# Windowed attention on one core: value products of three blocks in one run, a written order for the tensor engine, and the query projection spread over the blocks

## Chip, core and metric

The kernel is one program on one core of a Trainium2 chip. The core has a tensor engine (PE, whose weight loads the profile lists apart as PEld), a vector engine (DVE), a scalar engine (ACT), GpSimd (POOL), and a sync engine (SP) whose queue issues the DMA transfers here. Each engine works through its own instructions in order, and semaphores tie them together. Operands lie in the on-chip memory SBUF; PE writes to PSUM, eight banks of 128 partitions by 512 floats, and DVE and ACT read PSUM back.

The metric is device time of one execution in microseconds, the median of several runs. The profile is of one execution, with the time of every instruction.

## The reference

Two sequences, a prompt of 256 positions and a sample of 512, go through a network of two layers of width 1024. Layer 0 mixes with a chunked mLSTM, layer 1 with windowed attention, and each is followed by a feed-forward part with a short convolution. All is float32. The change lies in the attention of layer 1:

```python
def swa_mixer(h, w_in, sink, rel_bias, w_out):
    proj = h @ w_in
    q, k, v = ...        # 16 query heads, 4 key/value heads, 64 wide
    ...
    def block(i):        # 128 query positions, keys of up to 384 positions around them
        s = jnp.einsum('bqkgd,bckd->bkgqc', qb, kb).astype(jnp.float32) * scale + bias
        s = jnp.where(valid, s, -jnp.inf)
        m = jnp.maximum(jnp.max(s, axis=-1, keepdims=True), sink_l)
        p = jnp.exp(s - m)
        denom = jnp.sum(p, axis=-1, keepdims=True) + jnp.exp(sink_l - m)
        ob = jnp.einsum('bkgqc,bckd->bqkgd', p / denom, vb.astype(jnp.float32))
        return ob.astype(h.dtype)
    ...
    return outs @ w_out
```

## The kernel before

The two sequences stand side by side as 768 columns, the prompt in columns 0 to 255 and the sample in 256 to 767. Float32 matrices that go through PE at full rate are split into a high and a low part in a reduced format, and a product is three matmuls: high by high, high by low, low by high (line 268, `gemmT_steps`). A projection of 128 output rows over one sequence is eight steps of three matmuls, 512 columns wide for the sample and 256 for the prompt, into one PSUM bank.

The attention stage is `swa` (line 814). It projects the keys and the first half of the queries (`window`, line 283), multiplies a one-hot matrix with the table of relative biases (line 862) and sends the result to memory, from where the bias rows `bt` are loaded for each pair of heads (line 913). The values are projected by `gemmN` (line 304) into `vn`. The queries come in eight halves of 128 rows, one for each pair of heads j: weights are loaded in halves of 512 KB (`raw`) and split by ACT (`whi`, line 232) and DVE (`wlo`, line 233). What a projection leaves in PSUM is scaled and split for each of the two heads by ACT (line 852) and DVE (line 853).

The attention itself is a list of 48 blocks: eight pairs of heads, for each the four blocks of the sample and the two of the prompt. A block has 128 query positions and 256 or 384 keys. It goes through three functions:

- `scores` (line 906): four matmuls, two for each head, into two banks; DVE adds the bias and takes the maximum (line 929), ACT takes the exponentials with their sum (line 938), DVE forms the reciprocal of the sum (line 943), POOL scales the probabilities `t` (line 945).
- `flip` (line 947): PE transposes the probabilities by 128 columns at a time (line 953), four or six transposes, and ACT and DVE copy them to `pt` (lines 957 and 955).
- `values` (line 959): products of the transposed probabilities with `vn`. Each head of a pair fills 64 of the 128 rows of the result, so these matmuls use 64 columns of the array, all others 128. A bank `po` collects the blocks of one sequence, and ACT copies it to `att` behind the last of them (line 974).

`pack` (line 885) splits a finished pair of heads for the output projection, ACT the high part and DVE the low one. It writes over `hh` and `hl`, the input that the query projections read.

The loop at line 979 writes, for step x, the scores of block x, three steps of the query projection of a later unit, the flip of block x-3 (`LAG`, line 36) and the values of block x-4. It does not fix the order on the engines. A scheduler does: it takes instructions by their place in the program and by when its own estimate of times has them ready, engine by engine. So the matmuls stand on PE in another order than they are written, and matmuls of the output projection (`out_proj`, line 559), which comes next in the program, stand among the blocks as well.

PSUM is held as two groups of four banks. `ps` (line 207) serves the projections. `pa` (line 213) serves scores, flips, and `po`.

SBUF holds six large tiles (`slab`): keys, query halves, attention outputs, and, toward the end of the stage, the residual input that the output projection adds to, loaded in six transfers of 512 KB.

Of the kernel before, what the change touches and what calls it, by code (L numbers as in the profile page):

```python
# [10 lines left out]
F32 = mybir.dt.float32  # L11
# [4 lines left out]
P = 128  # L16
# [17 lines left out]
NPART = FC // 2  # L34
EPS = 1e-6
LAG = 3

HELD = float("inf")
BIG = 1.0e30
# [24 lines left out]
U_AIN = 20  # L64
# [77 lines left out]
class Net:  # L142
# [671 lines left out]
    def swa(self, pool):  # L814
# [26 lines left out]
        def queries(u, c):  # L841
            if c == 0:
                qts[u] = self.slab([P, 4, T], R)
            qt = qts[u]

            def evac(q, o):
                s0, s1 = SEQS[q]
                for e in range(2):
                    src = o[64 * e : 64 * e + 64]
                    hi = qt[64 * e : 64 * e + 64, 2 * c + e, s0:s1]  # L850
                    lo = qt[64 - 64 * e : 128 - 64 * e, 2 * c + e, s0:s1]
                    nc.scalar.activation(hi, src, AF.Copy, scale=0.125)
                    nc.vector.scalar_tensor_tensor(lo, src, 0.125, hi.bitcast(F32), ALU.mult, ALU.subtract)

            return evac

        items = [(w, keys(c)) for c, w in self.halves(U_AIN)]
        rest = self.halves(U_AIN + 2)
# [9 lines left out]
        v = pool.tile([P, T // P, 256], F32, name="vn")  # L868
        self.gemmN(U_AIN + 1, lambda t, o: nc.scalar.copy(v[:, t], o))

        _, w = next(rest)
        evac = queries(0, 1)
        for q in range(2):
            evac(q, self.gemmT(w, q))
        att = [self.slab([P, 4, T]) for _ in range(2)]

        def project(u):
            for c, w in self.halves(U_AIN + 2 + u):
                evac = queries(u, c)
                for q in range(2):  # L880
                    for o in self.gemmT_steps(w, q):
                        yield
                    evac(q, o)

        def pack(c):
            for s0, s1 in SEQS:
                self.fp_copy_split(self.hh[:, c, s0:s1], self.hl[:, c, s0:s1], att[c // 4][:, c % 4, s0:s1])
# [4 lines left out]
        blocks = []  # L892
        for j in range(8):
            for q, (s0, s1) in enumerate(SEQS):
                n = (s1 - s0) // P
                for i in range(n):
                    b = Block()
# [6 lines left out]
        po = {}  # L904

        def scores(b):
            j, kv = b.j, b.j // 2
            if j not in bias:
                bias[j] = []
                for e in range(2):  # L910
                    bt = pool.tile([P, 384], F32, tag="bt", name=self.nm("bt"), bufs=3)
                    row = bd[2 * j + e : 2 * j + e + 1]
                    nc.sync.dma_start(
                        bt, bass.AP(tensor=row.tensor, offset=row.offset, ap=[[1, P], [1, 384]])
                    )
                    bias[j].append(bt)
            co = (b.lo - b.i + 1) * P
            k0 = b.s0 + b.lo * P
            q0 = b.s0 + b.i * P
            K = b.K  # L920
            b.t = t = pool.tile([P, 2, 384], F32, tag="t", name=self.nm("t"), bufs=4)
            st = pool.tile([P, 8], F32, tag="st", name=self.nm("st"), bufs=6)
            rm, mx, sm, rd = (st[:, 2 * z : 2 * z + 2] for z in range(4))
            for e in range(2):
                S = self.pa()[:, :K]
                qb = qts[j // 2][:, 2 * (j % 2) + e, q0 : q0 + P]
                for z in range(2):
                    self.mm(S, qb, kk[kv // 2][:, kv % 2, z, k0 : k0 + K], z == 0, z == 1)
                nc.vector.tensor_tensor_reduce(
                    out=t[:, e, :K], in0=S, in1=bias[j][e][:, 384 - co - K : 384 - co][:, ::-1], op0=ALU.add, op1=ALU.max,  # L930
                    scale=1.0, scalar=-BIG, accum_out=rm[:, e : e + 1],
                )
            sk = self.cst(SK + 2 * j, 2)
            nc.vector.tensor_tensor(mx, rm, sk, ALU.max)
            nc.vector.tensor_tensor(rd, sk, mx, ALU.subtract)
            nc.vector.tensor_scalar(mx, mx, -1.0, None, ALU.mult)
            for e in range(2):
                nc.scalar.activation(
                    t[:, e, :K], t[:, e, :K], AF.Exp, bias=mx[:, e : e + 1], accum_out=sm[:, e : e + 1]
                )  # L940
            nc.scalar.activation(rd, rd, AF.Exp)
            nc.vector.tensor_tensor(rd, rd, sm, ALU.add)
            nc.vector.reciprocal(rd, rd)
            for e in range(2):
                nc.gpsimd.tensor_scalar(t[:, e, :K], t[:, e, :K], rd[:, e : e + 1], 1.0, ALU.mult, ALU.mult)

        def flip(b):
            b.pt = pool.tile([P, 2, 384], F32, tag="pt", name=self.nm("pt"), bufs=3)
            for e in range(2):
                pp = self.pa()[:, : b.K]  # L950
                for kb in range(b.nk):
                    ks = slice(kb * P, (kb + 1) * P)
                    nc.tensor.transpose(pp[:, ks], b.t[:, e, ks], self.ident)  # L953
                if e:
                    nc.vector.tensor_copy(b.pt[:, e, : b.K], pp)
                else:
                    nc.scalar.copy(b.pt[:, e, : b.K], pp)

        def values(b):
            j, kv = b.j, b.j // 2  # L960
            if b.i == 0:
                po[j, b.q] = self.pa()
            o = po[j, b.q]
            for kb in range(b.nk):
                for e in range(2):
                    self.mm(
                        o[64 * e : 64 * e + 64, b.i * P : (b.i + 1) * P],
                        v[:, b.s0 // P + b.lo + kb, kv * 64 : (kv + 1) * 64],
                        b.pt[:, e, kb * P : (kb + 1) * P],
                        kb == 0,  # L970
                        kb == b.nk - 1,
                    )
            if b.i == b.n - 1:
                nc.scalar.copy(att[j // 4][:, j % 4, b.s0 : b.s1], o[:, : b.s1 - b.s0])

        fill = iter(())
        nb = len(blocks)
        packed = 0
        for x in range(nb + LAG + 1):
            if x < nb:  # L980
                if x % 12 == 0:
                    for _ in fill:
                        pass
                    u = x // 12 + 1
                    fill = project(u) if u < 4 else iter(())
                scores(blocks[x])
            for _ in range(3):
                next(fill, None)
            if LAG <= x < nb + LAG:
                flip(blocks[x - LAG])  # L990
            if x > LAG:
                b = blocks[x - LAG - 1]
                values(b)
                if x >= 36 and b.i == b.n - 1 and b.q == 1:
                    while packed <= b.j:
                        pack(packed)
                        packed += 1
        return None


# [596 lines left out]
```

## Time and profile before

| | us |
|---|---|
| median of 3 runs | 1900.98 |
| lowest and highest of them | 1899.35, 1902.82 |
| the profiled execution | 1904.33 |
| its span, first to last instruction | 1902.5 |

| engine | busy us | share of the span | instructions |
|---|---|---|---|
| PE | 1830.7 | 96% | 11270 |
| PEld | 1667.5 | 88% | 11270 |
| DVE | 1399.1 | 74% | 2296 |
| ACT | 910.3 | 48% | 1832 |
| POOL | 490.3 | 26% | 387 |

The attention stage runs from about 1080 to 1290 us; the output projection and the feed-forward part of layer 1 follow to the end.

How to read the lines: a group is named by source line, engine, operation and out<-in tiles (buffer numbers left out), with partitions by elements; behind the count stand busy time and mean duration, then the idle time of the engine before the group and what ended it. In a timeline the first two columns are start and length. A matmul's length covers its way through the array, and the next one starts before it ends. So PE counts as busy nearly all the time, and its pace is read from one start to the next. A float32 product with both operands unsplit, such as a value product, is recorded as two matmuls.

### The profile page before, as it was taken

Reading aid. Unit: us, or ns where it says so; the run is one execution under the profiler, and the core shown is the slowest. Engines: PE = TensorE matmul, PEld = TensorE weight load, DVE = VectorE, ACT = ScalarE, POOL = GpSimd, SP = SyncE. Lnnn points to the kernel's source line nnn. Section 1 sums busy time; section 2 is a strip of 40 time slices with the busy share of each in tenths; the row PEclk is TensorE's granted clock in tenths of the full one; section 3 lists DMA queues with packets and bytes.
Section 4 is the critical chain, followed back from the end, with each engine's and each line's share of the span. In section 5 each row is a group of like instructions: output and inputs, shape, how many; then the busy total and the mean of one; then the engine's idle time right before and its main releaser. Section 6 shows DMA issues by size and latency. Waiting matters only on the chain. (4 is left out here: it accounts for less than half of the span.)

```text
span 1902.5 us, 29053 instructions
## 1 busy us (share of the span) xinstructions
PE 1830.7 (96%) x11270; PEld 1667.5 (88%) x11270; DVE 1399.1 (74%) x2296; ACT 910.3 (48%) x1832; POOL 490.3 (26%) x387
## 2 busy tenths in 40 slices
PE   7999999999999999999999999999989999999997
PEld 4987887888998999999999998779979999999997
DVE  4665577686689777777777755875997777777776
ACT  3444433444455444444444555774565444444443
POOL 2101001031023333333332211340133333333322
PEclk9999999999999999999999999999999999999998
DMA  8343556556312222222223221122222222222211
GB/s 330 109 134 121 167 181 195 168 164 208 99 53 69 68 67 67 67 67 67 67 67 100 90 89 43 44 85 89 78 78 78 67 67 67 67 67 67 67 34 67
DMA packets 64245, 184.48 MB, mean 97 GB/s; under 512 B 6167, under 2 KB 23831, under 8 KB 64108
## 3 DMA queue, kind: packets, MB, share of 16 engines
q1 hardware_dynamic: 64108, 182.63, 29.6%
q8 instruction: 88, 1.44, 0.3%
q14 instruction: 49, 0.40, 0.1%
HBM read 176.17 MB, written 6.43 MB: 96 GB/s over the span
## 5 line engine op out<-in xcount | busy, mean ns | idle before, releaser
L232 ACT CAST whi<-raw 128x1024 fp32r<-128x1024 f32 x237 | 248.5, 1049 | 412.2 <-PE pa L226 197.9
L233 DVE TENSOR_TENSOR wlo<-raw,whi 128x1024 fp32r<-128x1024 f32 x237 | 325.2, 1373 | 123.9 <-ACT whi L232 122.8
L226 PE MATMUL pa<-slab,whi 128*128 128x256 f32 (+1 forms) x1472 | 348.8, 334 | 4.7 <-DVE slab L557 4.5
L226 PEld LDWEIGHTS pa<-slab,whi 128*128 128x128 f32 x1472 | 254.0, 191 | 31.6 <-DVE slab L557 6.4
L557 DVE SCALAR_TENSOR_TENSOR slab<-pa,mod,slab 128x256 f32<-128x256 f32 (+1 forms) x368 | 207.6, 591 | 72.7 <-PE pa L226 72.3
L226 PE MATMUL pa<-slab,wlo 128*128 128x256 f32 (+1 forms) x736 | 235.4, 332 | 0.0
L226 PE MATMUL ps<-zh,whi 128*128 128x256 f32 (+2 forms) x688 | 228.8, 336 | 4.6 <-ACT whi L232 3.5
L226 PE MATMUL ps<-zh,wlo 128*128 128x256 f32 (+2 forms) x688 | 229.1, 336 | 4.0 <-DVE wlo L233 4.0
L226 PE MATMUL ps<-zl,whi 128*128 128x256 f32 (+2 forms) x688 | 229.4, 335 | 0.4 <-DVE zl L520 0.4
L1114 PE MATMUL ps<-zh,whi 128*128 128x384 f32 x504 | 171.1, 339 | 15.8 <-ACT ps L1169 14.5
L1115 PE MATMUL ps<-zl,whi 128*128 128x384 f32 x504 | 169.7, 337 | 0.8 <-DVE zl L1072 0.8
L1116 PE MATMUL ps<-zh,wlo 128*128 128x384 f32 x504 | 168.9, 335 | 0.0
L226 PEld LDWEIGHTS pa<-slab,wlo 128*128 128x128 f32 x736 | 140.2, 191 | 13.4 <-DVE wlo L233 0.9
L226 PEld LDWEIGHTS ps<-zh,whi 128*128 128x128 f32 x688 | 132.0, 193 | 17.5 <-ACT whi L232 5.1
L226 PEld LDWEIGHTS ps<-zh,wlo 128*128 128x128 f32 x688 | 132.2, 192 | 15.1 <-DVE wlo L233 4.8
L226 PEld LDWEIGHTS ps<-zl,whi 128*128 128x128 f32 x688 | 132.2, 193 | 11.5 <-issue 1.7
L1367 POOL TENSOR_TENSOR slab<-slab 128x772 f32<-128x772 f32 x44 | 83.7, 1903 | 205.0 <-DVE slab L1341 193.5
L1145 POOL TENSOR_TENSOR raw<-raw,raw 128x512 f32<-128x512 f32 x40 | 52.3, 1308 | 293.9 <-DVE wlo L233 244.3
L1340 DVE SCALAR_TENSOR_TENSOR slab<-slab,cstt,slab 128x771 f32<-128x771 f32 x88 | 104.8, 1193 | 26.9 <-ACT slab L1338 26.9
L1341 DVE SCALAR_TENSOR_TENSOR slab<-slab,cstt,slab 128x771 f32<-128x771 f32 x88 | 120.2, 1365 | 0.8
L476 DVE SCALAR_TENSOR_TENSOR ada<-raw,silc,ada 128x1024 f32<-128x1024 f32 x84 | 112.4, 1369 | 7.7 <-DMA raw<-in_adaln_w_dram 7.5
L1114 PEld LDWEIGHTS ps<-zh,whi 128*128 128x128 f32 x504 | 94.6, 188 | 23.9 <-ACT ps L1169 19.7
(291 smaller groups left out, 4155.0 us busy)
## 6 DMA issues: line engine op xcount, KB each, us to landing
raw<-in_w_dram SPq DMA_DIRECT2D x208, 512.0 KB, 3.7
raw<-in_adaln_w_dram SPq DMA_DIRECT2D x84, 512.0 KB, 4.3
slab<-in_x_dram SPq DMA_DIRECT2D x12, 512.0 KB, 7.6
slab<-in_adaln_w_dram SPq DMA_DIRECT2D x12, 512.0 KB, 10.3
slab<-mrows SPq DMA_DIRECT2D x8, 384.0 KB, 5.7
xs<-slab SPq DMA_DIRECT2D x6, 512.0 KB, 3.7
bt<-brow SPq DMA_DIRECT2D x16, 192.0 KB, 3.1
slab<-xs SPq DMA_DIRECT2D x6, 512.0 KB, 9.0
```

The source lines that it names most:

```text
L226: self.nc.tensor.matmul(out, lhsT, rhs, start=start, stop=stop)
L232: nc.scalar.copy(hi, src)
L233: return nc.vector.tensor_tensor(lo, src, hi.bitcast(F32), ALU.subtract)
L476: stt(acc[:, s], row, w, acc[:, s], ALU.mult, ALU.add)
L557: self.nc.vector.scalar_tensor_tensor(x, o, self.mod[l][:, gc + c, q : q + 1], x, ALU.mult, ALU.add)
L1114: mm(o, wh[:, k], hi[k], start=start and k == 0, stop=False, skip_group_check=True)
L1115: mm(o, wh[:, k], lo[k], start=False, stop=False, skip_group_check=True)
L1116: mm(o, wl[:, k], hi[k], start=False, stop=k == 3, skip_group_check=True)
L1145: tt(q[0], q[2], q[0], ALU.subtract)
L1340: stt(y[:, 1:], u[:, :-1], w(0), y[:, 1:], ALU.mult, ALU.add)
L1341: stt(y[:, :-1], u[:, 1:], w(2), y[:, :-1], ALU.mult, ALU.add)
L1367: nc.gpsimd.tensor_tensor(y, y, yrow[:, j], ALU.mult)
```

## The change

- The loop's PE instructions stand in a block with a written order: PE takes them as the program lists them, and no other PE work comes between. The other engines are still ordered by the scheduler.
- The values of three blocks are written together, in every third step, right behind that step's flip.
- The bank `po` comes from `ps`, the projections' group, in place of `pa`.
- `pt` has five buffers in place of three.
- The seven halves of the queries behind the first are one generator of 113 steps with the weights fetched and split one half ahead. The second half, which was projected ahead of the loop, is part of it. Step x of the loop runs it on until 6 + (x+1)*107/40 steps (rounded down, at most 113) are done, so it ends at x = 39.
- The call of `gemmT` for the second half goes, and with it its `tick`, which hands time to pending normalizations; at that point there is none.

In the written order of the changed kernel a step is: the projection's matmuls, the scores of block x, the flip of block x-3, and every third step the values of blocks x-6 to x-4. Value products form 16 runs on PE where they form 74 before. Before, 63 matmuls of the output projection stand ahead of the last value product; after the change none does. POOL has the same instructions in the same order. On SP the same 386 transfers are issued, eleven weight loads, bias rows and residual loads among them in another order.

```diff
-        _, w = next(rest)
-        evac = queries(0, 1)
-        for q in range(2):
-            evac(q, self.gemmT(w, q))
         att = [self.slab([P, 4, T]) for _ in range(2)]
 
-        def project(u):
-            for c, w in self.halves(U_AIN + 2 + u):
-                evac = queries(u, c)
+        def weights():
+            yield next(rest)[1]
+            for u in range(1, 4):
+                for _, w in self.halves(U_AIN + 2 + u):
+                    yield w
+
+        def project():
+
+            ws = weights()
+            nxt = next(ws)
+            for j in range(1, 8):
+                w, nxt = nxt, next(ws, None)
+                evac = queries(j // 2, j % 2)
                 for q in range(2):
                     for o in self.gemmT_steps(w, q):
                         yield
...
-            b.pt = pool.tile([P, 2, 384], F32, tag="pt", name=self.nm("pt"), bufs=3)
+            b.pt = pool.tile([P, 2, 384], F32, tag="pt", name=self.nm("pt"), bufs=5)
...
-                po[j, b.q] = self.pa()
+                po[j, b.q] = self.ps()
...
-        fill = iter(())
+        fill = project()
         nb = len(blocks)
-        packed = 0
-        for x in range(nb + LAG + 1):
-            if x < nb:
-                if x % 12 == 0:
-                    for _ in fill:
-                        pass
-                    u = x // 12 + 1
-                    fill = project(u) if u < 4 else iter(())
-                scores(blocks[x])
-            for _ in range(3):
-                next(fill, None)
-            if LAG <= x < nb + LAG:
-                flip(blocks[x - LAG])
-            if x > LAG:
-                b = blocks[x - LAG - 1]
-                values(b)
-                if x >= 36 and b.i == b.n - 1 and b.q == 1:
-                    while packed <= b.j:
-                        pack(packed)
-                        packed += 1
+        packed = done = 0
+        with self.tc.manual_schedule(engines={mybir.EngineType.PE}):
+            for x in range(nb + LAG + 1):
+
+                while done < min(113, AHEAD + (x + 1) * (113 - AHEAD) // 40):
+                    next(fill, None)
+                    done += 1
+                if x < nb:
+                    scores(blocks[x])
+                if LAG <= x < nb + LAG:
+                    flip(blocks[x - LAG])
+                if x > LAG and (x - LAG) % GROUP == 0:
+                    for b in blocks[x - LAG - GROUP : x - LAG]:
+                        values(b)
+                    if x >= 36 and b.i == b.n - 1 and b.q == 1:
+                        while packed <= b.j:
+                            pack(packed)
+                            packed += 1
```

`GROUP` is 3 and `AHEAD` is 6; `LAG` stays 3.

More of the change, by code (lines that the diff above doesn't have):

```diff
@@ L36 @@
 LAG = 3
+GROUP = 3
+AHEAD = 6
 HELD = float("inf")
```

## The prediction

> **What bounds the kernel now.** I read the page first, then the chain of waits of the attention stage, then its stretches, its matmul groups and the tensor engine's (PE's) timeline. The page:
>
> ```profile
> span 1902.5 us, 29053 instructions
> ...
> PEclk9999999999999999999999999999999999999998
> ```
>
> The clock is granted in full. The chain of waits cut to 1200:1290 us, the later half of the stage that the change touches, lies on PE for over 99%:
>
> ```profile
> by line: PE pa L226 57.6%; PE pa L953 27.1%; PE ps L226 14.6%; ACT zh L232 0.5%; ACT slab L974 0.4%; issue 0.2%
> ```
>
> Stretches (columns: stretch, its us, busy us and instructions of PE, PEld, DVE, ACT, POOL, granted clock, DMA share, GB/s): the stage up to its last value product, its late part, and the kernel's end.
>
> ```profile
> 1085.35:1289.00 203.65, 203.48 (x1479) 167.20 (x1478) 141.27 (x560) 128.61 (x386) 51.96 (x98) 1.00 0.21 63
> 1240.00:1285.00 45.00, 44.95 (x339) 33.74 (x339) 35.07 (x181) 34.24 (x120) 17.40 (x34) 1.00 0.24 75
> 1880.00:1902.00 22.00, 12.48 (x74) 11.93 (x74) 9.74 (x25) 6.28 (x17) 5.66 (x8) 0.69 0.36 119
> ```
>
> PE looks full, but these durations overlap. What PE can do is read from starts that follow each other. The matmul groups of the first stretch, by shape:
>
> ```profile
> L226 PE MATMUL pa<-pt,vn 128*64 128x128 f32 x448 | 46.4, 287 | 0.0
> L953 PE MATMUL pa<-kct,t 128*128 128x128 f32 x224 | 40.4, 283 | 0.1
> L226 PE MATMUL pa<-slab,slab 128*128 128x256 f32 x128 | 25.9, 304 | 0.0
> L226 PE MATMUL ps<-zh,wlo 128*128 128x512 f32 x56 | 22.5, 401 | 0.0
> ```
>
> Value products (`pt,vn`) take 64 columns of the array, all others 128. PE's timeline around one run of them:
>
> ```profile
> 1133.82 0.81 PE L953 MATMUL pa<-kct,t 128*128 128x128 f32 x6
> ...
> 1135.17 0.40 PE L226 MATMUL ps<-zh,wlo 128*128 128x512 f32 x1
> 1135.50 0.66 PE L226 MATMUL pa<-pt,vn 128*64 128x128 f32 x8
> 1136.08 0.50 PE L226 MATMUL ps<-zh,whi 128*128 128x512 f32 x1
> 1136.42 0.40 PE L226 MATMUL ps<-zl,whi 128*128 128x512 f32 x1
> 1136.66 0.40 PE L226 MATMUL pa<-slab,slab 128*128 128x256 f32 x2
> 1136.89 0.39 PE L226 MATMUL ps<-zh,wlo 128*128 128x512 f32 x1
> ```
>
> A 512-wide matmul costs 0.23 us (1136.89 on is 1136.66 plus two 256-wide ones, 0.12 each). Six transposes in 0.81 us give (0.81 - 0.27) / 5 = 0.109 each. Value records start in pairs, the two heads side by side, a pair in 0.109. But entering the run takes 0.33 where 0.23 is due, the run with its exit 0.58 where four pairs are 0.44, and the first matmul behind it 0.34 where 0.23 is due: 0.35 us for one trip to 64 columns and back; without the slow matmul behind it, which a short transpose there may show less of, 0.24. I take **0.32 us a trip**, near the full one that the rows show. The weight loads bear the count of trips out:
>
> ```profile
> L226 PEld LDWEIGHTS pa<-pt,vn 128*64 128x64 f32 x448 | 28.4, 136 | 13.0 <-issue 7.7 <-DVE st L929 1.3 <-DVE st L934 0.7
> ```
>
> The written order of the built kernel has 74 runs of value products, and the loads of their weights were preceded by 13.0 us of idle time, 0.18 a run.
>
> **The sum for before.** From the bias product (1085.35) to the first output-projection matmul behind the last value product (1289.80, below) pass 204.45 us. Due by counts of the written order: 509 matmuls of 256 columns x 0.1195, 168 of 512 x 0.23, 127 of 384 x 0.1735, 224 transposes and 224 pairs of value records x 0.109, the bias product 0.96: 171.2 us. Over it: 33.25, of which 74 x 0.32 = 23.7 are trips, 0.7 lies at the bias product, 1.0 at the end, and 7.85 are value products without a partner and waits for the softmax. The end:
>
> ```profile
> 1289.80 0.79 PE L226 MATMUL ps<-zh,whi 128*128 128x384 f32 x3 [0.90 <-ACT zh L232]
> ...
> 1290.96 0.33 PE L226 MATMUL ps<-zh,wlo 128*128 128x384 f32 x1
> 1291.13 0.33 PE L226 MATMUL ps<-zl,whi 128*128 128x384 f32 x1
> 1291.31 0.34 PE L226 MATMUL ps<-zh,wlo 128*128 128x384 f32 x1
> 1291.90 0.44 PE L226 MATMUL ps<-zh,whi 128*128 128x384 f32 x1 [0.26 <-ACT whi L232]
> ...
> 1294.26 0.40 PE L226 MATMUL ps<-zh,wlo 128*128 128x384 f32 x1
> ```
>
> Here three output tiles, filled side by side, end together, and the next three wait for their weights: from 1291.31 to 1294.26 seven starts in 2.95 us where 7 x 0.174 = 1.22 are due, 1.73 lost.
>
> **The change, part by part.** No matmul is added or removed.
>
> *Grouping.* The written order has 16 value runs instead of 74: 58 trips x 0.32 = 18.6 us saved, and heads stay paired, so most of the 7.85 goes too. Bounds: 0.24 to 0.35 a trip, and nothing to all of the 7.85.
>
> *Output projection.* 63 matmuls of 384 columns, fill among the blocks today, go behind the last value product: 63 x 0.1735 = 10.9 us that stay in the sum. They now run tile after tile, so the wait for the last packed chunk (1.0) and the weight wait (1.73) are hidden by other tiles.
>
> *A fixed PE order.* Each of 51 steps has its share of projection, scores of block x, transposes of x-3, and every third step the values of three blocks. If a block's softmax is late, PE waits and all behind it. With projections, six blocks cost PE (16 steps of three matmuls, 8.4; scores 3.3, transposes 3.05, values 3.05, two trips 0.64) 18.4 us; from scores to the same block's transposes the order puts three steps, 8.6 us in the tightest place (scores, transposes and values of its own step 2.98, two steps of 2.21, projection 0.72 and scores 0.48 of the third) and up to 10.8. The softmax chain, first reduce to the end of the scaling on POOL, for a block amid dense projections and a late one:
>
> ```profile
> 1190.59 0.55 DVE L929 CUSTOM_DVE_ANT_0 t<-pa,bt 128x384 f32<-128x384 f32 x1
> ...
> 1197.94 1.16 POOL L945 TENSOR_SCALAR t<-t,st 128x384 f32<-128x384 f32 x2 [6.24 <-ACT pt L957]
> ...
> 1271.80 0.56 DVE L929 CUSTOM_DVE_ANT_0 t<-pa,bt 128x384 f32<-128x384 f32 x1
> ...
> 1277.64 1.15 POOL L945 TENSOR_SCALAR t<-t,st 128x384 f32<-128x384 f32 x2 [3.39 <-DVE st L936]
> ```
>
> 8.5 and 7.0 us, and 0.35 from the scores to the reduce: 7.35 fits, 8.85 misses by 0.25 in the tightest place, at most 2 us over seven times six blocks. I take 1. At the start only 5.2 us lie between the first scores and their transposes: 7.35 - 5.2, **2 us**.
>
> *The last sixteen steps* have projections only for four and nothing to fill with behind them; PE's due there, from block 33's scores on and by the same prices, is 37.8 us. The late stretch above holds 18 blocks:
>
> ```profile
> L938 ACT ACTIVATE t<-t,st 128x256 f32<-128x256 f32 x24 | 12.0, 503 | 1.1 <-DVE st L943 1.0
> L938 ACT ACTIVATE t<-t,st 128x384 f32<-128x384 f32 x12 | 7.3, 607 | 0.0
> ...
> L232 ACT CAST zh<-slab 128x512 fp32r<-128x512 f32 x3 | 1.9, 620 | 0.1
> ...
> L232 ACT CAST zh<-slab 128x256 fp32r<-128x256 f32 x3 | 1.2, 391 | 0.0
> ```
>
> ACT's 34.24 us less three packings of 1.01 are 1.73 a block, and DVE's 35.07 are of the same size. Blocks 33 to 47 with the copies of two earlier ones are 15.5 x 1.73 = 26.8; all eight packings fall here, since they overwrite what the projections read, 8.1; the last half's evictions and two weight casts about 4: 38.9 us on ACT. It begins 1.9 us behind block 33's scores, and 0.5 of products follow its last copy. Always busy, ACT ends PE's part at 41.3; at 90% at 45.6; at today's 76% at 53.6. Over 37.8: 3.5, 7.8, 15.8. I take **8**, since the written order keeps ACT fed by three blocks at once.
>
> *Queues.* The eleven weight and bias loads on SP that stand among these steps are reordered, bias rows ahead of weights; weight splits stand two halves ahead of their use, some 18 us. POOL's order is the same. The value banks now come from the projections' four, of which two and two are live at most; the copied probabilities have five buffers for three. I cost all three at nothing, hidden by those 18 us; a bias row that is late by its landing would cost DVE about 1 us in each six blocks, inside the slack above except in the last eight.
>
> **Sum.** 171.2 + 16 x 0.32 + 0.7 + (2 + 1 + 8) = 188.0 against 204.45, so 16.4; with the weight wait 18.1 us. Span 1902.5 - 18.1 = 1884.4; the profiled run of 1904.33 would be 1886.2; the median of the runs, 1900.98, lies 3.35 below that run and becomes **1883**.
>
> The ends: waits of 0 + 0 + 3.5 give 18.1 + 7.5 = 25.6 (1875.4); waits of 2 + 2 + 15.8 and nothing of the 7.85 give 18.1 - 8.8 - 7.85 = 1.4 (1899.5), and with trips at 0.24 besides, -3.2 (1904), which I leave out of the range.
>
> **Rivals.**
> *ACT keeps today's share at the end.* The last steps wait 15.8 instead of 8, the chain in the middle 2: gain 18.1 - 8.8, 1891 to 1892. For it: 76% is what ACT reaches now; against: today nothing presses it, as PE sets the pace.
> *The trip's price hangs on the products, not on the run.* Then 58 fewer trips give nothing: 18.1 - 18.6, 1901. Against: the rows show it only at a run's ends.
> *The fixed order is paced by the softmax: slower.* Place: transposes of x-3. From a chain of 10.3 us with its lead, kept up, the gain is gone (48 x 10.3 / 3 = 165 against 137.8 due, 2 at the start included). At 11.4, the 8.85 above and 2.5 more for a weight cast and an eviction queued ahead of the exponentials, 48 x 3.8 = 182.4, and the kernel takes 1918. Against: both are in the 8.5 already.
> *The clock drops in the last steps.* The kernel's end above shows 0.69 where PE works 12.48 of 22 us. At that share 17.3 us of matmuls (blocks 40 on) take 7.8 longer: 1891. Against: my waits there are 1 to 3 us with work between. [...]
>
> **How the numbers follow.** Forecast 0.60 (own range 1877 to 1891), an even larger gain 0.05, ACT's share 0.16, the clock 0.04, no trip saving 0.07, softmax-paced 0.08. Range 1875 to 1897: it leaves out the last two. 0.2% is 3.8 us, about what can be told from no change: faster 0.85, same 0.07, slower 0.08.
>
> **What would show it.** Right: 16 stretches of value products, PE's stage shorter by 16 us to the same point, idle PE before transposes only in the last dozen steps, ACT over 85% there, no triple weight wait. Wrong: transposes waiting for POOL in the middle; a late bias row on DVE; matmuls behind value runs that still start 0.34 apart more than 16 times; granted clock under 1.

## The result, and the profile after

The changed kernel takes 1889.78 us (median of 7 runs beside 1899.35 for the kernel before): ratio 0.9941, interval 0.9924 to 0.9958. That is 9.6 us less by the medians and 11.2 by the ratio, where 18 were forecast. A second set of runs gave 0.9948, 0.9932 to 0.9964. The first execution that was profiled was a disturbed one of 4343.1 us, which the ratio leaves out, so all lines of "after" are from another execution of the same kernel, of 1891.66 us. Line numbers there are those of the changed kernel: L230, L939, L948, L955 and L963 were L226, L929, L938, L945 and L953 before. Its page:

```profile
span 1889.5 us, 29064 instructions
...
PEclk7999999999999999999999999999999999999998
```

The span is 13.0 us shorter. Where that lies is read at three instructions that both kernels have: the bias product, and the 64th and the 151st 384-column matmul of the output projection (before, 63 of them stand ahead of the last value product, so that the 64th is the first one behind it). PE's timeline after:

```profile
1084.79 1.03 PE L230 MATMUL pa<-oh,rb 33*16 33x512 f32 x2
...
1269.04 0.44 PE L230 MATMUL ps<-zh,whi 128*128 128x384 f32 x1 [0.73 <-ACT slab L984]
...
1280.09 0.33 PE L230 MATMUL ps<-zh,whi 128*128 128x384 f32 x1
...
1295.17 0.33 PE L230 MATMUL ps<-zh,whi 128*128 128x384 f32 x1
```

and the 151st before (its 64th is the row at 1289.80 in the prediction):

```profile
1306.81 0.33 PE L226 MATMUL ps<-zh,whi 128*128 128x384 f32 x1
```

From the bias product to the 64th, 204.45 us became 195.30: 9.15 won, 16.4 forecast. From there to the 151st, 17.01 became 15.08: the weight wait, 1.93 for the forecast 1.73. That is 11.1 us; the other 1.9 us of the span lie ahead of the bias product (0.56) and behind the 151st (1.36), where the change moves no matmul. So one term came in almost whole, and 7.25 us are missing in the stage.

The stage's chain of waits, cut to 1200:1269 us, has changed its nature. Before, PE held over 99% of it:

```profile
by line: PE ps L230 16.7%; DVE t L939 14.1%; ACT t L948 10.2%; DMA bt<-brow 9.4%; issue 7.9%; DVE zl L237 6.6%; DVE pt L965 5.1%; PE pa L963 4.6%; DVE wlo L237 3.3%; DVE slab L857 2.9%; DVE st L946 2.6%; ACT zh L236 2.5%; DVE st L945 2.5%; 
```

`DMA bt<-brow`, the bias rows, was costed at nothing. PE's groups in the stage: transposes now have idle time before them (0.1 us before), and the weight loads of value products have 2.7 us of it instead of 13.0, still 0.17 a run, for 16 runs:

```profile
L963 PE MATMUL pa<-kct,t 128*128 128x128 f32 x224 | 36.3, 284 | 6.2 <-DVE st L946 2.4 <-DVE st L952 1.4 <-DVE st L944 1.2
```

```profile
L230 PEld LDWEIGHTS ps<-pt,vn 128*64 128x64 f32 x448 | 24.1, 137 | 2.7 <-issue 2.7
```

One run of value products in the middle:

```profile
1152.19 0.60 PE L963 MATMUL pa<-kct,t 128*128 128x128 f32 x4
1152.72 1.97 PE L230 MATMUL ps<-pt,vn 128*64 128x128 f32 x32
1154.62 0.39 PE L230 MATMUL ps<-zh,whi 128*128 128x256 f32 x1
1154.84 0.28 PE L230 MATMUL ps<-zl,whi 128*128 128x256 f32 x1
1154.96 0.28 PE L230 MATMUL ps<-zh,wlo 128*128 128x256 f32 x1
```

Into the run 0.53 where four transposes are 0.44; the run 1.90 where 16 pairs are 1.74; the 256-column matmul behind it 0.22 where 0.12 is due: 0.35 us a trip, and no more for 16 pairs than for four. By counts, the stage after is due 160.3 us; of the 23.95 above it, 16 trips are 5.6, the bias product 0.15, the start (scores of blocks 0 to 5) 2.4, the middle (blocks 6 to 35) 3.8, and everything from the scores of block 36 on 12.0 us. "Waits" below means this: time from start to start less the prediction's counts and 0.35 a run.

The late rows. Waits of DVE in the stage (line, waited for: us in total, times, longest), after and then before:

```profile
DVE t L939 <- DMA bt<-brow: 6.1, 7, 1.2
```

```profile
DVE t L929 <- DMA bt<-brow: 1.4, 1, 1.4
```

How one comes about, in DVE's and SP's timelines after:

```profile
1246.56 0.42 DVE L939 CUSTOM_DVE_ANT_0 t<-pa,bt 128x256 f32<-128x256 f32 x1
1246.91 0.42 DVE L939 CUSTOM_DVE_ANT_0 t<-pa,bt 128x256 f32<-128x256 f32 x1
...
1248.77 0.42 DVE L939 CUSTOM_DVE_ANT_0 t<-pa,bt 128x256 f32<-128x256 f32 x1
...
1250.04 0.42 DVE L939 CUSTOM_DVE_ANT_0 t<-pa,bt 128x256 f32<-128x256 f32 x1 [0.77 <-DMA bt<-brow]
```

```profile
1247.02 0.32 SPq L923 DMA_DIRECT2D bt<-brow  x1
```

Three buffers hold one and a half head pairs. The last head pair's second row can be fetched only when the first reduce of block 41 (1246.56) has let go of a buffer; issued at 1247.02 it is there at 1250.04, and the reduce of block 42 for it stands 0.77 us. All of DVE's queue stands behind that reduce. PE feels it at the banks: in the middle of the stage, 1131:1235 us, its score matmuls (L230 into `pa`) wait for a reduce to free one. The part of it that shows as idle time of PE:

```profile
PE pa L230 <- DVE st L939: 0.6, 2, 0.4
```

The last steps, in PE's timeline and in stretches with the columns of the prediction's:

```profile
1241.40 0.74 PE L230 MATMUL pa<-slab,slab 128*128 128x256 f32 x4
1244.52 1.46 PE L963 MATMUL pa<-kct,t 128*128 128x128 f32 x6 [2.38 <-DVE st L946]
1245.64 1.20 PE L230 MATMUL pa<-slab,slab 128*128 128x256 f32 x4
1246.73 1.51 PE L963 MATMUL pa<-kct,t 128*128 128x128 f32 x6
```

```profile
1218.90:1268.03 49.13, 43.33 (x380) 35.81 (x380) 41.21 (x181) 38.98 (x128) 19.84 (x36) 0.97 0.22 67
```

```profile
1245.10:1248.40 3.30, 3.30 (x15) 3.15 (x16) 2.65 (x16) 2.91 (x12) 1.75 (x4) 0.50 0.07 22
```

From behind block 33's scores to the last value product DVE is busy for 84%, ACT for 79%: neither is full. And after a wait of 2.38 us the granted clock is 0.50 for 3.4 us; four 256-column matmuls take 1.20 us there, 0.74 just before.

### The profile page after: what moved, and what is told of

It reads as the page before. It is cut to its first block, busy times and chain, and to the rows that moved or that the text cites. A ratio compares the mean times of both kernels' runs of the same rounds, so it can differ in the third digit from the quotient of the medians.

```text
span 4341.1 us, 29064 instructions
## 1 busy us (share of the span) xinstructions
PE 4313.3 (99%) x11270; PEld 3393.3 (78%) x11270; DVE 1353.5 (31%) x2296; ACT 924.1 (21%) x1832; POOL 424.5 (10%) x387
## 4 chain that ended last, share of the span: by engine, by line
PE 99%; ACT 0%; DMA 0%; POOL 0%; DVE 0%; issue 0%; SPq 0%; POOLq 0%; DVEq 0%; ACTq 0%
PE ps L230 33%; PE pa L230 28%; PE ps L1122 11%; PE ps L1124 11%; PE ps L1123 11%; PE pa L963 2%; PE pa L1124 1%; PE pa L1123 1%; PE pa L1122 1%; PE pa L796 0%; PE ps L495 0%; DMA slab<-in_x_dram 0%; POOL slab L550 0%; ACT nt L108 0%; ACT whi L236 0%
## 5 line engine op out<-in xcount | busy, mean ns | idle before, releaser
L230 PE MATMUL pa<-slab,whi 128*128 128x256 f32 (+1 forms) x1472 | 742.0, 627 | 0.0
L230 PEld LDWEIGHTS pa<-slab,whi 128*128 128x128 f32 x1472 | 501.9, 371 | 137.8 <-issue 127.3
L230 PE MATMUL ps<-zh,whi 128*128 128x256 f32 (+2 forms) x688 | 458.0, 667 | 2.7 <-ACT whi L236 2.2
L230 PE MATMUL ps<-zh,wlo 128*128 128x256 f32 (+2 forms) x688 | 453.4, 663 | 0.0
L230 PE MATMUL ps<-zl,whi 128*128 128x256 f32 (+2 forms) x688 | 451.0, 657 | 0.0
L230 PE MATMUL pa<-slab,wlo 128*128 128x256 f32 (+1 forms) x736 | 445.9, 621 | 0.0
L230 PEld LDWEIGHTS ps<-zh,whi 128*128 128x128 f32 x688 | 265.4, 387 | 75.8 <-issue 65.2
L230 PEld LDWEIGHTS ps<-zh,wlo 128*128 128x128 f32 x688 | 269.8, 392 | 67.2 <-issue 63.2
L230 PEld LDWEIGHTS pa<-slab,wlo 128*128 128x128 f32 x736 | 273.2, 371 | 61.9 <-issue 56.6
L230 PEld LDWEIGHTS ps<-zl,whi 128*128 128x128 f32 x688 | 266.1, 388 | 61.1 <-issue 59.8
L1122 PEld LDWEIGHTS ps<-zh,whi 128*128 128x128 f32 x504 | 174.4, 346 | 47.1 <-issue 32.0
L1124 PEld LDWEIGHTS ps<-zh,wlo 128*128 128x128 f32 x504 | 173.1, 343 | 43.2 <-issue 37.2
L1123 PEld LDWEIGHTS ps<-zl,whi 128*128 128x128 f32 x504 | 168.5, 334 | 44.2 <-issue 38.9
L1122 PE MATMUL ps<-yh,whi 128*128 128x384 f32 x304 | 200.2, 658 | 0.0
```

The lines of the kernel that those rows point to most:

```text
L230: self.nc.tensor.matmul(out, lhsT, rhs, start=start, stop=stop)
L1122: mm(o, wh[:, k], hi[k], start=start and k == 0, stop=False, skip_group_check=True)
L1123: mm(o, wh[:, k], lo[k], start=False, stop=False, skip_group_check=True)
L1124: mm(o, wl[:, k], hi[k], start=False, stop=k == 3, skip_group_check=True)
```

## Experiments

All ratios are against the kernel before, run beside them. "Stage" is from the bias product to the first output-projection matmul behind the last value product, as read from each kernel's timeline; "to the 64th" is from the bias product to the 64th matmul of the output projection; it counts the 63 moved matmuls in every kernel, and so compares all of them. (The expectations call this matmul the 63rd.)

| kernel | value runs | stage us | to the 64th us | waits from block 36 us | ratio, interval |
|---|---|---|---|---|---|
| before | 74 | 204.45 | 204.45 | 3.3 | 1 |
| after, again | 16 | 184.25 | 195.30 | 12.0 | 0.9948, 0.9932 to 0.9964 |
| values a block at a time | 47 | 189.37 | 200.39 | 10.1 | 0.9964, 0.9952 to 0.9975 |
| no written order | 89 | 203.71 | 214.74 | 7.8 | 1.0042, 1.003 to 1.0054 |
| four row buffers | 16 | 180.64 | 191.69 | 12.1 | 0.9903, 0.9887 to 0.9919 |
| packings left out | 16 | 179.78 | 190.81 | 7.5 | 0.9912, 0.9898 to 0.9927 |
| lag of four | 16 | 180.96 | 191.99 | 9.6 | 0.9926, 0.9912 to 0.994 |
| split runs | 38 | 189.66 | 200.71 | 12.9 | 0.9966, 0.9953 to 0.998 |
| filled wait | 16 | 184.29 | 195.33 | 11.2 | 0.9926, 0.9907 to 0.9945 |
| lag of four, four rows | 16 | 181.11 | 192.17 | 13.0 | 0.9917, 0.9897 to 0.9936 |
| the same, packings in turns | 16 | 181.13 | 192.19 | 13.0 | 0.9912, 0.9892 to 0.9933 |
| free tail, old banks there, four rows | 18 | 187.44 | 187.44 | 7.3 | 0.9908, 0.989 to 0.9927 |
| no order, old banks | 26 | 192.68 | 192.68 | 5.5 | 0.9939, 0.9925 to 0.9952 |

**The same kernel, values a block at a time, and no written order.**

> The changed kernel once more, for an undisturbed profile. The trip theory (0.32 us a run of value products, 16 runs) puts the last value product 160.3 + 5.1 + 0.7 = 166.1 us of due work behind the bias product, and what is over that are new waits. The gain of 11 us where 18 were forecast leaves some 18 us of new waits instead of 11. If ACT paces the end, the extra 7 lie in the last sixteen steps and PE's idle time there is before transposes that wait for POOL. If the softmax paces the middle, six blocks take more than 18.4 us between steps 6 and 35. If the price of a trip was read too high, neither stretch shows waits and the matmuls behind value runs start closer together.

```diff
-GROUP = 3
+GROUP = 1
```

> Values of one block at a time in the written order: 47 runs of value products instead of 16, the same products and the same pairs. If a run costs 0.32 us, 31 more cost 9.9 us and the ratio to before goes from 0.994 to about 0.999. If the price hangs on the products and not on the run, the time stays at 0.994.

```diff
-        with self.tc.manual_schedule(engines={mybir.EngineType.PE}):
+        if True:
```

> The change without the written order: values still grouped by three in the program, bank, spread projection and buffers as changed, the scheduler orders PE again. It makes 89 runs of value products. Trip theory: 73 runs more than the changed kernel cost 23 us, against which stand the waits that the written order brings (11 to 18 us): ratio 0.997 to 1.001. If the written order itself is what held the gain back, this one is faster than the changed kernel, below 0.990.

A value run per block costs 5.1 us of stage for 31 more runs, 0.16 each: half of what the rows say. Without the written order the rest of the change is slower than before, with 89 runs. The split runs settle the first below, the value banks the second.

**A fourth row buffer.**

```diff
-                        bt = pool.tile([P, 384], F32, tag="bt", name=self.nm("bt"), bufs=3)
+                        bt = pool.tile([P, 384], F32, tag="bt", name=self.nm("bt"), bufs=4)
```

> A fourth buffer for the bias rows, nothing else. The changed kernel's stage (bias product to the first output projection behind the last value product) took 184.25 us, its six-block periods in the middle 19.1 to 19.6 us, where a kernel with a run of values per block has 0.3 us of waits besides its trips, this one 0.7 to 1.2. Theory (late bias rows): the reduce waits seven times, 6.1 us in all, for a row that can only be fetched when the row of the head pair before is free; with a fourth buffer these waits go, the middle periods fall to 18.7 to 19.0, the last steps gain up to 1 us: stage 180.5 to 182.5. Rival (the wait is inside the slack; the middle waits come from the values of three blocks standing together): the waits on the rows go, the periods stay within 0.15 us, stage 183.7 to 184.8.

```profile
DVE t L939 <- PE pa L230: 12.0, 18, 3.5
```

This is the only entry of the reduce among DVE's waits now: none waits for a row, and no score matmul of PE waits for a reduce any more. The transposes of block 6 and of block 30, four periods of six blocks apart, after and with the fourth buffer:

```profile
1141.63 0.74 PE L963 MATMUL pa<-kct,t 128*128 128x128 f32 x4
...
1218.89 0.73 PE L963 MATMUL pa<-kct,t 128*128 128x128 f32 x4
```

```profile
1140.76 0.60 PE L963 MATMUL pa<-kct,t 128*128 128x128 f32 x4
...
1214.75 0.60 PE L963 MATMUL pa<-kct,t 128*128 128x128 f32 x4
```

A period is 19.3 us after and 18.5 here; 18.55 was forecast (18.4, and a seventh of the 1 us of waits). The stage is 3.6 us shorter; nothing is won from block 36 on, where the clock now drops twice. The late rows are the middle's whole excess. This version is faster than both kernels.

**Packings left out; a lag of four; split runs.**

```diff
-                            pack(packed)
                             packed += 1
```

> The packing of the attention output (eight chunks, on ScalarE and VectorE) is left out, so that the output projection multiplies what the projections read. Theory (packings): they stand among the exponentials and reduces of blocks 33 to 42 and stretch the softmax chain from 5 to 6.8 us to 9 to 10; without them the chain stays under 7 us, the waits from block 33's scores on fall from 12.5 us to 4 to 6: stage 176 to 178.5. Rival (latency: three steps without projections are shorter than any chain): the waits fall by under 3 us, stage over 181.5. Either way the last of the ScalarE work before the output projection is gone, up to 0.7 us more.

```diff
-LAG = 3
+LAG = 4
...
-            b.t = t = pool.tile([P, 2, 384], F32, tag="t", name=self.nm("t"), bufs=4)
+            b.t = t = pool.tile([P, 2, 384], F32, tag="t", name=self.nm("t"), bufs=5)
...
-            b.pt = pool.tile([P, 2, 384], F32, tag="pt", name=self.nm("pt"), bufs=5)
+            b.pt = pool.tile([P, 2, 384], F32, tag="pt", name=self.nm("pt"), bufs=4)
```

> Transposes follow the scores by four steps instead of three (five score tiles for four, four probability tiles for five). Theory (latency): the chain has one step more, 2.2 to 3.2 us; the start's wait falls from 2.8 us to under 1, the last steps' 12.5 us to 6 to 8: stage 177 to 180. Rival (the late bias rows and the packings set the end, ScalarE and VectorE have too much work there): only the start and the middle gain, stage 181.5 to 183.5.

```diff
                     for b in blocks[x - LAG - GROUP : x - LAG]:
+                        if b is not blocks[x - LAG - GROUP]:
+                            next(fill, None)
+                            done += 1
                         values(b)
```

> One step of the projection is put between the values of the three blocks of a group: 38 runs of value products for 16, all else as in the changed kernel. Theory (a trip costs 0.30 us wherever it stands): 22 x 0.30 = 6.6 us, stage 190 to 191.5, or 188 to 190 where it eats into the waits of the middle (3 us at most). Rival (a trip costs half of that, as the 31 extra runs of the one-block kernel with 5.1 us seem to say): stage 187 to 188.

The packings are worth 4.5 us of the 12.0, nearly all of it between the scores of blocks 36 and 42; 7.5 remain, so both theories of that run hold a part. In this kernel the clock does not drop, and up to 1.7 of the 4.5 can be that (half of the 3.4 us at 0.50). The lag takes the start's wait away (2.4 us to 0.1) and 2.4 us of the end's; the rows are late all the same, seven times, and the middle's waits rise from 3.8 us to 5.1. The split runs settle the price of a trip. Block 6's and block 30's transposes there and in the kernel with a run per block:

```profile
1141.88 0.68 PE L963 MATMUL pa<-kct,t 128*128 128x128 f32 x4
...
1221.87 0.73 PE L963 MATMUL pa<-kct,t 128*128 128x128 f32 x4
```

```profile
1138.79 0.60 PE L963 MATMUL pa<-kct,t 128*128 128x128 f32 x4
...
1218.35 0.60 PE L963 MATMUL pa<-kct,t 128*128 128x128 f32 x4
```

20.0 and 19.9 us a period, both with six runs. Against 18.5 with two runs and no late rows, four trips cost 1.4 to 1.5: 0.35 to 0.375 each, the price of the rows. Against the changed kernel's 19.3 they seem to cost half, because its late rows stand in the time that the trips would have taken: the split kernel's reduces wait six times for a row as well, 5.1 us in all, and PE's waits in its middle are 0.6 us.

**The wait filled.** Eight matmuls that nobody reads stand ahead of block 37's transposes, and count as work.

```diff
+        def warm(n):
+            if dummy[0] is None:
+                dummy[0] = self.ps()
+            for _ in range(n):
+                self.mm(dummy[0], kk[0][:, 0, 0, 0:128], kk[0][:, 0, 0, 0:512], True, True)
+
+        dummy = [None]
...
                     scores(blocks[x])
+                if x == LAG + 37:
+                    warm(8)
```

> Eight matmuls of 512 columns whose result nobody reads, 0.23 us each, stand in the one step where the changed kernel's transposes wait longest (block 37, 2.38 us idle; from 0.5 us after it the granted clock is 0.5 for 3.4 us). Theory (the clock costs time): the wait no longer lets the clock drop, the clock stays 1.0 through the last steps, and half of 3.4 us comes back: stage 182.3 to 183.3 us for 184.25. Rival (the softmax sets these steps, the slow matmuls only fill its waits): clock 1.0 there, stage 183.8 to 184.6. If the clock drops all the same, it does not hang on that wait.

```profile
1239.90 2.00 PE L230 MATMUL ps<-slab 128*128 128x512 f32 x8
1242.45 1.11 PE L963 MATMUL pa<-kct,t 128*128 128x128 f32 x6 [0.55 <-DVE st L946]
...
1259.06 1.11 PE L963 MATMUL pa<-kct,t 128*128 128x128 f32 x6 [1.03 <-POOL t L955]
1260.57 1.05 PE L963 MATMUL pa<-kct,t 128*128 128x128 f32 x4 [0.41 <-ACT t L948]
```

```profile
1261.20:1264.50 3.30, 3.30 (x30) 2.98 (x31) 1.05 (x5) 1.38 (x7) 1.95 (x6) 0.50 0.00 0
```

The clock stays up where it had dropped (blocks 36 to 41 are 0.6 us shorter) and drops seventeen microseconds later instead, counted from the bias product, behind two waits of 1.03 and 0.41 us; the last blocks give 1.6 us back. The stage is the same. What the clock costs in this kernel is not settled by it: at most half of 3.4 us, 1.7.

**Both cures, and the packings in turns.**

```diff
+                for _ in range(2):
+                    if x >= 40 and packed < ready:
+                        pack(packed // 2, packed % 2)
+                        packed += 1
```

> Four steps from scores to transposes and a fourth buffer for the bias rows together. With four steps alone the six-block periods of the middle held 1.63, 0.91, 1.21, 0.96 and 0.92 us of waits and seven late rows; with the fourth row buffer alone they held 0.1. Theory (both costs are separate and add): the five periods lose 5 us in all, stage 180.96 - 5 = 175.5 to 177 us. Rival (the rows' wait hides another of the same size at the end, where ScalarE and VectorE have fallen behind): the middle gains, the last twelve blocks give back over 2 us, stage over 178.

> As the kernel with four steps and four row buffers, and the packings are handed out two half chunks a step from step 40 on, instead of six chunks at once. Theory (packings hurt because they stand in front of many blocks' exponentials at once): blocks 36 to 41 lose most of the 4.2 us that leaving the packings out gained, the last blocks gain nothing: stage 173.5 to 176 us. Rival (only their total counts, and they now fall into the last steps, where nothing covers them): the same stage as without the drip or up to 2 us longer.

The rival holds: the middle gains (waits under 0.3 us in four of its five periods), the end loses 3.4 us to 13.0, with two drops of the clock in both kernels. The turns of the packings change nothing that the trace shows.

**The cover.** In the kernel before, 63 output-projection matmuls stand among the last blocks, and the waits from block 36 on are 3.3 us. Removing the written order alone does not bring these matmuls back among the blocks; with the value banks in their old place as well they are back. The value banks now come from the same four as the output projection's tiles, and those come after them in turn.

```diff
-                po[j, b.q] = self.ps()
+                po[j, b.q] = self.ps() if j < 6 else self.pa()
...
         with self.tc.manual_schedule(engines={mybir.EngineType.PE}):
-            for x in range(nb + LAG + 1):
+            for x in range(40):
+                step(x)
+        for x in range(40, nb + LAG + 1):
+            step(x)
```

> Four row buffers, the written order only for steps 0 to 39, and the value banks of the last two head pairs taken from the scores' banks as before; the built order then has 18 runs of value products and again 63 matmuls of the output projection ahead of the last of them. With four row buffers alone it has none there, the blocks from 36 on held 12.4 us of waits, and the 63rd output-projection matmul starts 191.7 us behind the bias product. Theory (the last blocks wait because the change took the output projection out of them, and it did so by the banks: the output projection's tiles take turns behind the last two value banks): the 63 matmuls, 10.9 us, stand in those waits, the 63rd starts after 183 to 186 us, waits from block 36 on 4 to 6 us, no drop of the clock there, ratio 0.986 to 0.988. Rival (the last blocks are set by ScalarE and VectorE, who also do the packings): the 63rd starts after 189 us or more, the waits only move.

```diff
-                po[j, b.q] = self.ps()
+                po[j, b.q] = self.pa()
```

(the second against the kernel without the order)

> No written order, even projection, five probability tiles, and the value banks where they were before (the scores' banks): one line from the kernel without the order. The built order has 26 runs for its 89, and 63 output-projection matmuls ahead of the last value product for its none. Theory (trips and cover make the difference): 63 fewer trips at 0.30 to 0.35 us and 6 to 8 us of waits at the end: from 214.7 us to the 63rd output-projection matmul to 185 to 192, ratio 0.989 to 0.993. Rival (the written order itself is what pays, through the even steps): over 198 us, ratio over 0.996.

With the banks back, the free tail has waits of 7.3 us for 12.1 and reaches the 64th 4.25 us earlier than with four row buffers alone: between theory and rival. It frees the order of the last steps and brings the banks back at once, and the kernel without any written order has waits of 7.8 us there with none of the 63 matmuls ahead. So the runs do not tell how much of the 4.8 us is the cover and how much the free order. But the output projection's three tiles then end together, and the wait for weights is back:

```profile
1271.92 0.44 PE L230 MATMUL ps<-zh,whi 128*128 128x384 f32 x1 [0.27 <-ACT whi L236]
1272.20 0.34 PE L230 MATMUL ps<-zl,whi 128*128 128x384 f32 x1
1272.87 0.44 PE L230 MATMUL ps<-zh,whi 128*128 128x384 f32 x1 [0.33 <-ACT whi L236]
```

The trace keeps 2.3 us of it at the 151st matmul, which the ratios (0.9908 and 0.9903) do not tell apart. The kernel without an order but with the old banks is the surprise. One line makes 89 runs 26 and brings 22.1 us to the 64th, and its ratio is that of the changed kernel. The idle time before the weight loads of value products, without the order and then with the old banks as well:

```profile
L230 PEld LDWEIGHTS ps<-pt,vn 128*64 128x64 f32 x448 | 30.0, 135 | 16.1 <-issue 12.3 <-DVE pt L965 1.0 <-ACT pt L967 0.2
```

```profile
L230 PEld LDWEIGHTS pa<-pt,vn 128*64 128x64 f32 x448 | 24.2, 136 | 4.5 <-issue 2.7 <-DVE st L944 0.7 <-ACT t L948 0.5
```

So the new banks need the written order, and the pair of them buys about what even steps and the old banks buy without it.

## Why the prediction was right, and where its sizes were off

The direction and the mechanism hold: trips are what the change saves. Term by term, forecast and measured:

- *A trip, 0.32:* 0.35, the upper of the two prices that the rows gave. 58 trips are 20.3 us, not 18.6; the 16 left cost 5.6, not 5.1 (+0.5).
- *Bias product, 0.7:* 0.15 (-0.55).
- *Start, 2 us:* 2.4 (+0.4); a lag of four removes it.
- *The middle, 1 us of waits by the softmax chain:* 3.8 (+2.8). The chain there is short, as argued: with a fourth row buffer 0.1 us of waits are left. The step that failed is the one on queues: a row "late by its landing would cost DVE about 1 us in each six blocks, inside the slack", costed at nothing. The size of the delay was right, 6.1 us over seven rows; the slack was not there. The reduce that stands for the row holds one of the four banks of scores and transposes, and DVE's queue. The fourth buffer removes 3.6 us.
- *The last steps, 8 us:* 12.0 from block 36 on (+4.0). ACT at 90% was the ground for 8; it reached 79%, DVE 84%. The rival with ACT's share of 76% foresaw 15.8. Neither engine is full: leaving the packings out takes 4.5 us away. What makes the other 7.5 is not settled; the length of the chain with little beside it is the likely cause, but a lag of four took 2.4 us off by itself and none together with the fourth row buffer. That the 63 moved matmuls "stay in the sum" was right, 11.05 us from 1269.04 to 1280.09. That they may also have been the cover of these steps was not priced; with them and a free order back there, the waits fall by 4.8 us, and the share of each is open.
- *The weight wait, 1.73:* 1.93, hidden as foreseen, and back as soon as the tiles end together.

The differences add to 7.15 of the 7.25 us missing.

Of the rivals, the softmax-paced order and the trip that saves nothing are refuted, by the time and by the split runs. The rival with ACT at today's share, 1891 to 1892, came nearer to the 1889.78 than the forecast of 1883. The share of 79% is what it had right; in part it was luck, as its 15.8 us at the end were too much and its 2 us for the middle, which knew of no late rows, too little. The clock did drop, to 0.50 for 3.4 us behind a wait of 2.38 us; the reason given for its small chance, waits of 1 to 3 us with work between, did not hold. Of what was to be seen, 16 runs, the missing weight wait and the idle transposes late in the stage are there; ACT over 85% is not, the stage is 9 us shorter at the same point and not 16, and two marks of a wrong step, a late row on DVE and a clock under 1, are there.

## What to carry to other kernels

Price every transfer whose buffer is freed by the instruction just ahead of its reader: landing time less the lead is the wait (for the last row here, 3.02 us less 2.25 is 0.77), and here one more buffer won as much as any of the reorderings tried. Before work is moved out of a stretch, ask what waits it may cover, and count the banks that let it stand there, since the scheduler's fill here hung on whose turn a bank was. Where two costs seem to be halves of what their rows say, look for a third that hides in the same time: here the late rows hid half of the trips.

## What the runs showed of the hardware that was not expected

The clock's drop does not follow from the length of a wait alone. In the changed kernel 2.38 us of idle PE were followed by 3.4 us at 0.50. With the wait filled, waits of 1.03 and 0.41 us were followed by the same. In the kernel with the free tail, a wait of 2.4 us was followed by none: its clock is at 1.00 from 1085 to 1310 us. Its waits of PE in the stage (the longest in the last column):

```profile
PE pa L963 <- POOL t L955: 2.6, 2, 2.4
```

In the changed kernel and with the wait filled the drop began when PE was at work again, 0.55 and 0.60 us behind the wait. With the split runs it began within a wait of 2.76 us, and lasted 6.8 us.

Nor does the drop follow from PE's busy time alone. In the 3.41 us ahead of it PE was busy for 1.03 us in the changed kernel and for 1.95 with the wait filled; with the free tail 3.5 us, from 1235.0 on, hold 1.11 us of busy PE, and no drop follows.

The times of the drops are alike. In the stage each lasts 3.41 us, in all kernels that have one, but for the 6.8 with the split runs. Where a kernel has two, they begin 17.07 us apart with four row buffers and with values a block at a time, 13.65 with a lag of four and four rows, and 13.66 with the packings in turns: five and four times 3.41. In the profiled execution of the kernel before, the clock is at 0.50 seven times, of which none is in the stage; the starts, from 38.18 to 1895.04 us, are 109.23, 170.67, 98.99, 631.47, 832.85 and 13.65 us apart, all whole multiples of 3.413. What makes the clock drop is not shown by these runs.
